# Moving convolutions, weights' products and a PSUM bank in the written order of a hybrid SSD/MLP mixer

## The chip, the core and the metric

The kernel runs on one core of a Trainium2 chip. The metric is the device time of one execution in microseconds (us). Three runs of the kernel before gave 1004.19, 1005.57 and 1009.1 us; their median, 1005.57 us, is the time before. The profile is of one further execution, which took 1003.8 us and whose recorded span is 1002.1 us, at a mean granted TensorE clock of 0.997.

Names of engines in the profile: PE is TensorE's matrix products, PEld its loading of weights, DVE is VectorE, ACT is ScalarE, POOL is GpSimd, SP is SyncE, which issues most DMAs.

## What is computed

One layer of a flow-matching backbone with 256 context tokens and 256 latent tokens, 2048 channels wide. One input projection feeds two groups of heads: a bidirectional Mamba-2 scan (SSD) and a chunked spatial-gating MLP. The part that matters here is the convolved half of the projection and the scan behind it (8 groups of 4 heads, chunks of 128 tokens):

```python
def _dwconv_rows(x, w, b, n_rows, row_len):          # 5 taps
    for k in range(CONV_W):
        y = y + xp[:, :, k:k + row_len] * w[k]
...
    xbc = jax.nn.silu(_dwconv_rows(z[..., :XBC_W], conv_w, conv_b, n_rows, row_len))
...
    states = jnp.einsum('bckgn,bckgr,bckgrp->bcgrpn', Bc, decay_to_end, xdt)
    CB = jnp.einsum('bcqgn,bckgn->bcgqk', Cc, Bc)
    Lmat = jnp.exp(jnp.where(mask, diff, -jnp.inf))
    y_diag = jnp.einsum('bcgqk,bcgrqk,bckgrp->bcqgrp', CB, Lmat, xdt)
    y_off = jnp.einsum('bcqgn,bcgrpn,bcqgr->bcqgrp', Cc, h_starts, jnp.exp(acs))
```

All of it is float32. The context's scans run once to give the start states of the latents' scans, and only latent tokens are put out.

## The kernel before

**Stages.** A prologue (adaLN vectors, RMSNorm, the projection of the time steps and the first seven column tiles) takes about 133 us. Then a loop over `REST` computes the other 25 column tiles of x, B and C, 128 channels each. A tile is numbered by its group and kind: tile 4g and 4g+1 are the two halves of the x channels of group g, 4g+2 is B, 4g+3 is C (C is needed for the latents alone and is 256 columns wide, the others 512). After it comes the "lat" stage, 16 blocks of 512 columns for z, u, v and z of the MLP, and then the output projection.

**Products.** Each float32 product is made of three products of split values (high by high, high by low, low by high). A weight half of 128x1024 arrives by DMA, ACT casts its high part (L414, `hi_w`) and DVE subtracts it to get the low part (L420, `lo_w`), three halves ahead of PE. A column tile takes 48 products (L138 to L140) into one PSUM bank `psx`. These banks come from a pool `acp` of two, in turn: tile n+2 of the loop writes the bank of tile n, once the convolution has read it. All other PSUM tiles come from a pool `sps` of six banks, which gives the bank that has been free longest.

**Convolution.** `conv_tile` makes the first tap on ACT (L479), the others on DVE (L495, eight instructions for a 512-wide tile and four for C), and silu on ACT (L498). Tiles 12, 13 and 15 were projected in the prologue, and wait in SBUF, in segments `zq` of the big buffer `y`; their taps read SBUF (`xbc<-y,...`), where the others read PSUM (`xbc<-psx,...`).

**Scan.** For x halves: `ptx` transposes (L614, PE) and the copy `xk` (L618, ACT); after the second half of a group come the weighted products `xw` (L626, POOL, four) and `xl` (L629, POOL, two), and the skip term (L742, POOL, `y<-xk,dsk`). For B: transposes `ptb` (L637, PE), copy `bk` (L642, ACT). For C: "states" on PE (`pcb` L680, `psc` L697, `psl` L700); `cbb` and `cbf` (L688, L689, DVE); `M` (L725 POOL, then L733 four times on DVE), `E` (L735, DVE), the carried state `hs` (copy L707 on ACT, L713 twice on POOL, `hl` L719 twice on DVE), and then `pso` (L750, PE), which reads `hs`; later `yo` (L756, DVE), `psy` (L776, PE), `pty` (L790, PE). The decays of the next group (L649 `R`, L662 `E` on ACT, with table loads) are queued in the same places. Letter and group are written together below: pso0 is the `pso` of group 0.

**What sets the order.** Every engine's queue stands in written order. Between products, `pump(dt)` advances a virtual clock (1.3 for six wide products, 0.65 for six 256-wide ones), and pieces that `later(dt, fn)` has queued are written when due. `plan_tile(i, src, d0, ds, tx, tw, late)` queues a tile's pieces: convolution at `d0`, silu at `d0 + ds`, transposes at `d0 + tx`; for the second x half `xw` and `xl` at `d0 + tx + tw` and the skip term 3 later; for C the whole list from states on, at `d0 + late` plus fixed offsets:

```python
        if r == 3:
            d0 += late
            for t, fn in [(6, ssd_cb), (6, ssd_states), (6.9, ssd_cbm), (7.6, lambda g: ssd_mb(g, 0)), (8, ssd_hc),
                          (8.7, ssd_hd), (9.4, lambda g: ssd_m(g, 0)), (10.2, ssd_hl), (11.2, lambda g: ssd_mb(g, 1)),
                          (12, ssd_o), (12.2, lambda g: ssd_m(g, 1)), (13.9, lambda g: ssd_yo(g, 0)),
```

The written order ends with block 0 of the lat stage, in which the last group's pieces stand. A block there takes two PSUM banks `pa`, of `acp` in even blocks and of `sps` in odd ones.

Of the kernel before, what the change touches and what calls it, by code (L numbers as in the profile page):

```python
# [8 lines left out]
F32 = mybir.dt.float32  # L9
# [6 lines left out]
P = 128  # L16
# [25 lines left out]
def tile_hybrid_ssd_mlp(  # L42
# [22 lines left out]
    def mkpool(**kw):  # L65
        return tc.tile_pool(reuse_waits="tile", **kw)
# [84 lines left out]
    def yseg(j):  # L151
        return y[:, j // 4, (j % 4) * 512 : (j % 4 + 1) * 512]


    zq = (yseg(2), yseg(3), yseg(7)[:, 0:256])
# [10 lines left out]
    acp = ctx.enter_context(mkpool(name="acp", bufs=2, space=PSUM))  # L166
    sps = ctx.enter_context(mkpool(name="sps", bufs=6, space=PSUM))

    def spt(shape, name):
        return sps.tile(shape, F32, tag="s", name=name)  # L170
# [116 lines left out]
    psx = []  # L287
# [161 lines left out]
    def later(dt, fn):  # L449
        queue.append((now[0] + dt, seq[0], fn))  # L450
        seq[0] += 1
# [14 lines left out]
    def conv_tile(i, src, d0, ds):  # L466
        ch = ORDER[i]
        lat = ch >= 24
        n = 256 if lat else 512
        cw = pc[:, C_CW + 5 * i : C_CW + 5 * i + 5]  # L470
        l0 = 0 if lat else 256
        T = {}

        def tap0():
            if ch < 16:
                o = cv3.tile([P, n], F32, tag="xs", name=f"xbc{i}")
            else:
                o = cv2.tile([P, n], F32, tag="cs" if lat else "bs", name=f"xbc{i}")
            nc.scalar.activation(o, src, AF.Identity, bias=pc[:, C_CB + i : C_CB + i + 1], scale=cw[:, 2:3])  # L479
            T["o"] = o  # L480

        def taps():
            o = T["o"]
            o4 = o[:, l0 : l0 + 256].rearrange("p (r t) -> p r t", r=4)
            src4 = src[:, l0 : l0 + 256].rearrange("p (r t) -> p r t", r=4)
            for k in (0, 1, 3, 4):
                s = k - 2
                parts = [(o4, src4, 64)]
                if not lat:
                    parts.append((o[:, 0:256], src[:, 0:256], 256))  # L490
                for (a, z, w) in parts:
                    o0, o1 = max(0, -s), w - max(0, s)
                    ao = a[..., o0:o1]
                    zi = z[..., o0 + s : o1 + s]
                    nc.vector.scalar_tensor_tensor(ao, zi, cw[:, k : k + 1], ao, op0=ALU.mult, op1=ALU.add)  # L495

        def silu():
            nc.scalar.activation(T["o"], T["o"], AF.Silu)  # L498
            done[i] = T["o"]

        later(d0, tap0)
        later(d0 + 0.9, taps)
        later(d0 + ds, silu)
# [102 lines left out]
    def ssd_x(g, xi):  # L606
        S = gs_.setdefault(g, {})
        if xi == 0:
            S["xk"] = cv2.tile([P, 4, 256], F32, tag="xk", name=f"xk{g}")
        xk = S["xk"]  # L610
        xt = done.pop(4 * g + xi)
        p = spt([P, 4, P], f"ptx{g}{xi}")
        for t in range(4):
            nc.tensor.transpose(p[:, t, :], xt[:, t * P : (t + 1) * P], ident)  # L614
        S["ptx", xi] = p

    def ssd_xc(g, xi):
        nc.scalar.copy(gs_[g]["xk"][:, :, xi * P : (xi + 1) * P], gs_[g]["ptx", xi])  # L618

    def ssd_w(g):  # L620
        S = gs_[g]
        xk, h4 = S["xk"], slice(4 * g, 4 * g + 4)
        xw = cv1.tile([P, 2, 2, 256], F32, tag="xw", name=f"xw{g}")
        for t in range(2):
            for d in range(2):
                nc.gpsimd.tensor_tensor(hp(xw[:, t, d, :]), hp(xk[:, t, :]), bc(wctx(t, d)[:, h4], 2, 64), op=ALU.mult)  # L626
        xl = cv1.tile([P, 2, 256], F32, tag="xl", name=f"xl{g}")
        for d in range(2):
            nc.gpsimd.tensor_tensor(hp(xl[:, d, :]), hp(xk[:, 2 + d, :]), bc(wlt(d)[:, h4], 2, 64), op=ALU.mult)  # L629
        S["xw"], S["xl"] = xw, xl  # L630
# [10 lines left out]
    def ssd_bc(g):  # L641
        nc.scalar.copy(gs_[g]["bk"], gs_[g]["ptb"])  # L642
# [153 lines left out]
    def plan_tile(i, src, d0=0.0, ds=5.2, tx=7.0, tw=1.5, late=0.0):  # L796

        g, r = divmod(i, 4)
        conv_tile(i, src, d0, ds)
        if r < 2:  # L800
            later(d0 + tx, lambda: ssd_x(g, r))
            later(d0 + tx + 0.7, lambda: ssd_xc(g, r))
        if r == 1:
            later(d0 + tx + tw, lambda: ssd_w(g))
            later(d0 + tx + tw + 3, lambda: ssd_sk(g))
        if r == 2:
            later(d0 + tx, lambda: ssd_b(g))
            later(d0 + tx + 0.7, lambda: ssd_bc(g))
# [5 lines that stand above are left out]
                          (14.5, lambda g: ssd_yo(g, 1)), (14.7, lambda g: ssd_ya(g, 0)), (15.3, lambda g: ssd_ya(g, 1)),  # L814
                          (16, ssd_yd), (16.9, ssd_yc), (18.6, ssd_yt), (19.3, ssd_yf)]:
                later(d0 + t, lambda fn=fn: fn(g))
            plan_d(d0 + 11, g + 1, 1.5)
            plan_e(d0 + 17, g + 1)
# [8 lines left out]
    later(2.5, lambda: nc.scalar.copy(zq[2], psx[6]))  # L827
    plan_tile(0, psx[0], 5, ds=7.5, tx=9.5)
    plan_tile(1, psx[1], 12.5, ds=8.5, tx=10)
    plan_tile(2, psx[2], 23.5, ds=7.5, tx=9.5)  # L830
    plan_tile(3, psx[3], 29, ds=5, late=1)
    plan_d(22, 0, 1.5)
    plan_e(27, 0)
    plan_tile(12, zq[0], 76, ds=7, tx=9)
    plan_tile(13, zq[1], 86, ds=7, tx=9)
    for n, i in enumerate(REST):
        lat = ORDER[i] >= 24
        ps = acp.tile([P, 256 if lat else 512], F32, tag="acc", name=f"psx{i}")
        for hf in range(2):
            whi, wlo = half(2 * n + hf)  # L840
            for kk in range(8):
                k = 8 * hf + kk
                w = slice(kk * P, (kk + 1) * P)
                mm3(ps, whi[:, w], wlo[:, w], k, k == 0, k == KT - 1, lat)
                if kk % 2:
                    pump(0.65 if lat else 1.3)
        if i < 8:
            plan_tile(i, ps, ds=7, tx=9, late=10)
        else:
            plan_tile(i, ps)  # L850
        if i == 14:
            plan_tile(15, zq[2], 6, late=10)

# [150 lines left out]
    base = 2 * len(REST)  # L1006
    for blk in range(16):
        kind, j4 = divmod(blk, 4)
        if blk % 2 == 0:
            pa = [acp.tile([P, 512], F32, tag="acc", name=f"pa{blk}{tk}") for tk in range(2)]  # L1010
        else:
            pa = [spt([P, 512], f"pa{blk}{tk}") for tk in range(2)]
        if kind == 1:
            later(3 if j4 == 0 else 0, lambda j4=j4: lat_vn(j4))
            later(10, lambda j4=j4: lat_sg(j4))
        for u in range(8):
            whi, wlo = half(base + blk * 8 + u)
            for kk in range(2):
                k = 2 * u + kk
                w = slice(kk * 512, (kk + 1) * 512)  # L1020
                for tk in range(2):
                    t = slice(256 + tk * P, 256 + (tk + 1) * P)
                    nc.tensor.matmul(pa[tk], lhsT=hhi[k][:, t], rhs=whi[:, w], start=k == 0, stop=False)  # L1023
                    nc.tensor.matmul(pa[tk], lhsT=hhi[k][:, t], rhs=wlo[:, w], start=False, stop=False)  # L1024
                    nc.tensor.matmul(pa[tk], lhsT=hlo[k][:, t], rhs=whi[:, w], start=False, stop=k == KT - 1)  # L1025
                pump(1.3)
            if blk == 0 and u == 7:
                pump(flush=True)
                man.close()
                pos[1] = max(halves) + 1  # L1030
                open_lat()
            if 1 <= blk < 9 and u % 4 == 1:
                gate_tile((blk - 1) * 2 + u // 4)
        if kind == 0:
            later(0, lambda j4=j4, pa=pa: lat_v(j4, pa))
        elif kind == 1:
            later(0, lambda j4=j4, pa=pa: lat_u(j4, pa))
        else:
            later(0, lambda kind=kind, j4=j4, pa=pa: lat_z(kind, j4, pa))
            for pair in range(2):  # L1040
                later(5 + 2 * pair, lambda kind=kind, j4=j4, pair=pair: lat_t(kind, j4, pair))
        if blk == 9:
            later(3, gate_bcast)
# [174 lines left out]
```

## Time and profile before

| what | number |
|---|---|
| median of three runs (lowest, highest) | 1005.57 us (1004.19, 1009.1) |
| profiled execution: time, span | 1003.8 us, 1002.1 us |
| weights' low parts in the loop, L420, DVE | 61 times, 1313 ns each |
| weights' high parts in the loop, L414, ACT | 61 times, 1043 ns each |
| taps from PSUM, L495, DVE | 204, 83.6 us in all |

How to read it: an engine's busy share says how much of the span it worked. A row of the timeline gives start and duration in us, engine, line, operation and tiles, the number of instructions in the row, and in brackets the engine's idle time ahead of it with what ended it. A PE row that begins with idle time in the loop or the lat stage is time in which no product ran.

### The profile page before, as it was taken

How to read it: one execution, taken by the hardware profiler on the slowest of the kernel's cores; microseconds unless marked ns; L12 is line 12 of the kernel's file. 1: busy time of each engine (PE TensorE's matmuls, PEld its weight loads, DVE VectorE, ACT ScalarE, POOL GpSimd, SP SyncE). 2: the span in 40 equal slices, each digit the busy share in tenths (PEclk: the TensorE clock that was granted, in tenths of full speed). 3: DMA queues.
4: the chain of work that ended last, by engine and by line, in shares of the span. 5: the costliest groups of instructions: out<-in, count | busy, mean ns of one | idle time of the engine just before them, and what ended most of it. 6: DMA issues, size and time to landing. Idle time of an engine off the chain costs nothing.

```text
span 1002.1 us, 14182 instructions
## 1 busy us (share of the span) xinstructions
PE 977.1 (98%) x5636; PEld 791.2 (79%) x5636; DVE 624.3 (62%) x944; ACT 492.9 (49%) x759; POOL 111.7 (11%) x162
## 2 busy tenths in 40 slices
PE   8999999999999999999999999999999999999996
PEld 3788887778687878777888888877888888888885
DVE  4344477777877665656667757666555564445546
ACT  4233347555656545544545334454565563446522
POOL 0000003423352222214000000000000000000000
PEclk9999999999999999999999999999999999999998
DMA  9999744233224323134878778674554545556722
GB/s 382 419 412 419 304 159 160 93 127 127 87 82 168 111 100 140 71 126 169 318 279 295 274 260 299 262 280 173 182 191 173 204 168 199 182 208 222 274 92 84
DMA packets 31554, 207.28 MB, mean 207 GB/s; under 512 B 4080, under 2 KB 4208, under 8 KB 7808
## 3 DMA queue, kind: packets, MB, share of 16 engines
q1 hardware_dynamic: 28656, 192.52, 51.1%
q0 software_dynamic: 2112, 12.65, 3.6%
q10 hardware_dynamic: 720, 1.20, 0.3%
q8 instruction: 44, 0.72, 0.3%
q14 instruction: 22, 0.18, 0.1%
HBM read 204.20 MB, written 2.16 MB: 206 GB/s over the span
## 4 chain that ended last, share of the span: by engine, by line
PE 71%; issue 10%; DMA 9%; DVE 7%; ACT 1%; POOL 1%; SPq 0%; DVEq 0%; POOLq 0%; ACTq 0%
PE psx L138 9%; PE psx L140 9%; PE psx L139 9%; PE pa L1023 5%; PE pa L1025 5%; PE pa L1024 5%; DMA gate<-in_wada_dram 5%; PE pm L1072 3%; PE pm L1071 3%; PE pm L1070 3%; PE psada L215 3%; DVE lo_w L82 2%; PE pq L1071 2%; PE pq L1072 2%; PE pq L1070 2%
## 5 line engine op out<-in xcount | busy, mean ns | idle before, releaser
L82 DVE TENSOR_TENSOR lo_w<-w,hi_w 128x1024 fp32r<-128x1024 f32 x173 | 210.1, 1223 | 136.5 <-ACT hi_w L81 136.4
L81 ACT CAST hi_w<-w 128x1024 fp32r<-128x1024 f32 x173 | 182.0, 1052 | 200.7 <-PE pa L1025 130.2
L1023 PE MATMUL pa<-hi_w,hhi 128*128 128x512 f32 x512 | 202.5, 396 | 2.1 <-DVE xbc L495 2.1
L1024 PE MATMUL pa<-lo_w,hhi 128*128 128x512 f32 x512 | 199.4, 390 | 0.1
L1025 PE MATMUL pa<-hi_w,hlo 128*128 128x512 f32 x512 | 199.5, 390 | 0.0
L138 PE MATMUL psx<-hhi,hi_w 128*128 128x512 f32 (+1 forms) x400 | 153.2, 383 | 0.0
L140 PE MATMUL psx<-hhi,lo_w 128*128 128x512 f32 (+1 forms) x400 | 146.0, 365 | 0.0
L139 PE MATMUL psx<-hlo,hi_w 128*128 128x512 f32 (+1 forms) x400 | 145.7, 364 | 0.0
L1023 PEld LDWEIGHTS pa<-hi_w,hhi 128*128 128x128 f32 x512 | 96.1, 188 | 23.1 <-issue 4.1
L1025 PEld LDWEIGHTS pa<-hi_w,hlo 128*128 128x128 f32 x512 | 96.1, 188 | 20.3
L495 DVE SCALAR_TENSOR_TENSOR xbc<-psx,pc,xbc 128x248 f32<-128x248 f32 (+1 forms) x204 | 83.6, 472 | 45.7 <-ACT xbc L479 44.7
L1024 PEld LDWEIGHTS pa<-lo_w,hhi 128*128 128x128 f32 x512 | 96.2, 188 | 19.9 <-DVE lo_w L82 0.5
L420 DVE TENSOR_TENSOR lo_w<-w,hi_w 128x1024 fp32r<-128x1024 f32 x61 | 79.6, 1313 | 21.6 <-ACT hi_w L414 21.6
L138 PEld LDWEIGHTS psx<-hhi,hi_w 128*128 128x128 f32 x400 | 75.5, 189 | 13.3 <-issue 2.8
L140 PEld LDWEIGHTS psx<-hhi,lo_w 128*128 128x128 f32 x400 | 75.4, 189 | 12.6
L139 PEld LDWEIGHTS psx<-hlo,hi_w 128*128 128x128 f32 x400 | 75.6, 189 | 12.0 <-issue 1.4
L414 ACT CAST hi_w<-w 128x1024 fp32r<-128x1024 f32 x61 | 63.5, 1043 | 29.3 <-PE psx L139 15.8
L884 DVE SCALAR_TENSOR_TENSOR junk<-gate,cb 128x2048 bf16<-128x2048 f32 x16 | 36.6, 2290 | 31.2 <-DMA gate<-in_wada_dram 31.1
L1070 PE MATMUL pm<-hi_w,hhi 128*128 128x512 f32 x128 | 49.9, 390 | 0.0
L1071 PE MATMUL pm<-lo_w,hhi 128*128 128x512 f32 x128 | 49.9, 390 | 0.0
L1072 PE MATMUL pm<-hi_w,hlo 128*128 128x512 f32 x128 | 49.7, 389 | 0.0
L138 PE MATMUL psx<-hhi,hi_st 128*128 128x512 f32 (+1 forms) x112 | 41.3, 368 | 0.0
(219 smaller groups left out, 1324.7 us busy)
## 6 DMA issues: line engine op xcount, KB each, us to landing
w<-in_wlat_dram SPq DMA_DIRECT2D x64, 1024.0 KB, 4.8
ada<-in_wada_dram SPq DMA_DIRECT2D x32, 1024.0 KB, 15.2
w<-in_wout_dram SPq DMA_DIRECT2D x32, 1024.0 KB, 4.8
w<-in_wxbc_dram SPq DMA_DIRECT2D x25, 1024.0 KB, 4.8
gate<-in_wada_dram SPq DMA_DIRECT2D x16, 1024.0 KB, 5.7
R<-acs POOLq DMA_DIRECT2D x8, 1024.0 KB, 5.2
wst<-in_wst_dram SPq DMA_DIRECT2D x16, 480.0 KB, 15.5
xT<-in_xch_dram SPq DMA_DIRECT2D x4, 1024.0 KB, 7.8
```

What stands on the lines that cost most here:

```text
L81: nc.scalar.copy(hi, raw)
L82: nc.vector.tensor_tensor(lo, raw, hi.bitcast(F32), op=ALU.subtract)
L138: nc.tensor.matmul(ps, lhsT=whi, rhs=hhi[k][:, s], start=start, stop=False)
L139: nc.tensor.matmul(ps, lhsT=whi, rhs=hlo[k][:, s], start=False, stop=False)
L140: nc.tensor.matmul(ps, lhsT=wlo, rhs=hhi[k][:, s], start=False, stop=stop)
L495: nc.vector.scalar_tensor_tensor(ao, zi, cw[:, k : k + 1], ao, op0=ALU.mult, op1=ALU.add)
L1023: nc.tensor.matmul(pa[tk], lhsT=hhi[k][:, t], rhs=whi[:, w], start=k == 0, stop=False)
L1024: nc.tensor.matmul(pa[tk], lhsT=hhi[k][:, t], rhs=wlo[:, w], start=False, stop=False)
L1025: nc.tensor.matmul(pa[tk], lhsT=hlo[k][:, t], rhs=whi[:, w], start=False, stop=k == KT - 1)
L1070: nc.tensor.matmul(p, lhsT=yh[:, t], rhs=whi[:, w], start=j == 0, stop=False)
L1071: nc.tensor.matmul(p, lhsT=yh[:, t], rhs=wlo[:, w], start=False, stop=False)
L1072: nc.tensor.matmul(p, lhsT=yl[:, t], rhs=whi[:, w], start=False, stop=hf == 0 and j == 15)
```

## The change

Six calls of `plan_tile` get other numbers, and the first two banks of the lat stage come from both pools. Tile 2's transposes are due 2 later; tile 3's list 1 later; tiles 12 and 13 are due 6 earlier and tile 13's transposes 1.5 later after its convolution; the second x half among tiles below 8 that the loop plans, which is tile 5 alone, has its weighted products and skip term 8.2 later; tile 15 is due 2 later. No instruction is added or taken away.

```diff
-    plan_tile(2, psx[2], 23.5, ds=7.5, tx=9.5)
-    plan_tile(3, psx[3], 29, ds=5, late=1)
+    plan_tile(2, psx[2], 23.5, ds=7.5, tx=11.5)
+    plan_tile(3, psx[3], 29, ds=5, late=2)
...
-    plan_tile(12, zq[0], 76, ds=7, tx=9)
-    plan_tile(13, zq[1], 86, ds=7, tx=9)
+    plan_tile(12, zq[0], 70, ds=7, tx=9)
+    plan_tile(13, zq[1], 80, ds=7, tx=10.5)
...
         if i < 8:
-            plan_tile(i, ps, ds=7, tx=9, late=10)
+            plan_tile(i, ps, ds=7, tx=9, tw=9.7, late=10)
...
         if i == 14:
-            plan_tile(15, zq[2], 6, late=10)
+            plan_tile(15, zq[2], 8, late=10)
...
-        if blk % 2 == 0:
+        if blk == 0:
+            pa = [acp.tile([P, 512], F32, tag="acc", name="pa00"), spt([P, 512], "pa01")]
+        elif blk % 2 == 0:
             pa = [acp.tile([P, 512], F32, tag="acc", name=f"pa{blk}{tk}") for tk in range(2)]
```

**POOL at group 0's states.** The rows from group 1's weighted products (`xw`, `xl` and the skip term `y`, all of `xk_1758`) to the second `M` of group 0. Before:

```order
L626 TENSOR_TENSOR xw_1912<-xk_1758,ed 128x256 x4
L629 TENSOR_TENSOR xl_1917<-xk_1758,ed 128x256 x2
L742 TENSOR_TENSOR y<-xk_1758,dsk 128x256 x2
L725 TENSOR_TENSOR M_2018<-cbb_2011,dtt 128x512
L713 TENSOR_TENSOR hs_2028<-hs_2028,ed 128x256 x2
L725 TENSOR_TENSOR M_2063<-cbb_2011,dtt 128x512
```

The same rows of the kernel after:

```order
L725 TENSOR_TENSOR M_2017<-cbb_2013,dtt 128x512
L626 TENSOR_TENSOR xw_2027<-xk_1758,ed 128x256 x4
L629 TENSOR_TENSOR xl_2032<-xk_1758,ed 128x256 x2
L713 TENSOR_TENSOR hs_2025<-hs_2025,ed 128x256 x2
L725 TENSOR_TENSOR M_2071<-cbb_2013,dtt 128x512
L742 TENSOR_TENSOR y<-xk_1758,dsk 128x256 x2
```

Group 0's first `M` passed all of group 1's products, and the skip term went behind group 0's pieces; `hs` still stands behind `xw` and `xl`.

**PE at the same place.** The end of tile 7 (`psx_1903`, 256 wide), group 0's states, and the first products of the next tile, tile 8, which is `psx_1999` before and `psx_1980` after. Before:

```order
L140 MATMUL psx_1903<-hhi_132,lo_w_1801 128x256
L680 MATMUL pcb_1990<-xbc_1883,xbc_1815 128x128 x2
L697 MATMUL psc_1993<-xw_1821,bk_1944 128x512 x2
L700 MATMUL psl_1996<-xl_1826,bk_1944 128x256 x2
L138 MATMUL psx_1999<-hhi_117,hi_w_1855 128x512
```

After:

```order
L140 MATMUL psx_1903<-hhi_132,lo_w_1801 128x256
L138 MATMUL psx_1980<-hhi_117,hi_w_1855 128x512
L139 MATMUL psx_1980<-hlo_133,hi_w_1855 128x512
L140 MATMUL psx_1980<-hhi_117,lo_w_1871 128x512
L138 MATMUL psx_1980<-hhi_118,hi_w_1855 128x512
L139 MATMUL psx_1980<-hlo_134,hi_w_1855 128x512
L140 MATMUL psx_1980<-hhi_118,lo_w_1871 128x512
L680 MATMUL pcb_1991<-xbc_1883,xbc_1815 128x128 x2
```

Six products of tile 8 now stand ahead of the states, which stood directly behind tile 7; the transposes `ptb` of group 0, some way above, moved 18 products down within tile 7.

**DVE at group 2's states.** The rows behind `cbb` and `cbf` of group 2. Before:

```order
L689 TENSOR_TENSOR cbf_2545<-pcb_2528,tri_le 128x256
L733 SCALAR_TENSOR_TENSOR M_2549<-cbf_2545,dtt,M_2549 128x128 x4
L735 TENSOR_TENSOR E_2347<-M_2549,E_2347 128x512
L719 TENSOR_TENSOR hs_2557<-psl_2534,hs_2557 128x256 x2
L495 SCALAR_TENSOR_TENSOR xbc_2582<-psx_2465,pc,xbc_2582 128x4x62
```

After, from the last two of the eight taps of tile 13 on (`xbc_2557`, read from `y`); the eight begin directly behind `cbf`:

```order
L495 SCALAR_TENSOR_TENSOR xbc_2557<-y,pc,xbc_2557 128x4x62
L495 SCALAR_TENSOR_TENSOR xbc_2557<-y,pc,xbc_2557 128x254
L733 SCALAR_TENSOR_TENSOR M_2559<-cbf_2552,dtt,M_2559 128x128 x4
L735 TENSOR_TENSOR E_2347<-M_2559,E_2347 128x512
L719 TENSOR_TENSOR hs_2567<-psl_2535,hs_2567 128x256 x2
```

Tile 13's taps passed group 2's `M`, `E` and `hs`, behind which they stood before.

**ACT there.** From the cast ahead of the copy `hs` of group 2. Before:

```order
L414 CAST hi_w_2526<-w_2341 128x1024
L707 COPY hs_2557<-psc_2531 128x2x256
L498 ACTIVATE xbc_2501<-xbc_2501 128x512
L479 ACTIVATE xbc_2582<-psx_2465,pc 128x512
L414 CAST hi_w_2584<-w_2341 128x1024
```

After:

```order
L414 CAST hi_w_2527<-w_2341 128x1024
L618 COPY xk_2538<-ptx_2539 128x4x128
L479 ACTIVATE xbc_2557<-y,pc 128x512
L707 COPY hs_2567<-psc_2532 128x2x256
L479 ACTIVATE xbc_2599<-psx_2475,pc 128x512
```

The copy `xk` of tile 12 and the first tap of tile 13 passed the copy `hs`; tile 12's silu (`xbc_2501`, `xbc_2434` after) went further up.

## The prediction

> **What bounds the kernel now.** I read the page first, then PE's waits, then the timeline round each wait.
>
> ```profile
> span 1002.1 us, 14182 instructions
> PE 977.1 (98%) x5636; PEld 791.2 (79%) x5636; DVE 624.3 (62%) x944; ACT 492.9 (49%) x759; POOL 111.7 (11%) x162
> ```
>
> PE works 98% of the span, and the change gives it no instruction more or less. So all that can be gained is PE's waits, and a wait removed early is kept to the end, since the engines behind PE are only 11 to 62% busy. The waits of PE (engine, line, what it waited for: us in total, times, longest):
>
> ```profile
> PE ptx L614 <- ACT xbc L498: 2.5, 1, 2.5
> PE pso L750 <- DVE hs L719: 2.2, 2, 2.0
> PE pa L1023 <- DVE xbc L495: 2.1, 1, 2.1
> ...
> PE ptb L637 <- ACT xbc L498: 1.3, 1, 1.3
> ```
>
> These four lines fit the four places of the change: `ptb` of tile 2, pso0, `ptx` of tile 13, and the second bank of the lat stage, pa01. PE's timeline there:
>
> ```profile
> 174.94 0.66 PE L637 MATMUL ptb<-ident,xbc 128*128 128x128 f32 x4 [1.28 <-ACT xbc L498]
> ...
> 188.94 0.39 PE L139 MATMUL psx<-hlo,hi_w 128*128 128x512 f32 x1
> 189.17 0.39 PE L140 MATMUL psx<-hhi,lo_w 128*128 128x512 f32 x1
> 191.53 1.96 PE L750 MATMUL pso<-hs,xbc 128*128 128x512 f32 x4 [1.97 <-DVE hs L719]
> ...
> 269.15 0.66 PE L614 MATMUL ptx<-ident,xbc 128*128 128x128 f32 x4 [2.47 <-ACT xbc L498]
> ...
> 443.83 0.47 PE L1023 MATMUL pa<-hi_w,hhi 128*128 128x512 f32 x1 [2.11 <-DVE xbc L495]
> ```
>
> Idle: 1.28 + 1.97 + 2.47 + 2.11 = 7.83 us. A stop costs a little more than its idle time: products start 0.23 apart (188.94, 189.17), pso0 started 2.36 behind the last, so 2.13 were lost for an idle 1.97, 0.16 more. Four stops lose 7.83 + 4 x 0.16 = 8.5. That is the most that can be gained. The fourth list is whether new waits take their place, so I follow each region through the new order, in the clock of before.
>
> **Region A, 173 to 192 us: ptb0, states, pso0.** `ptb0` stands 18 narrow products later, 18 x 0.12 = 2.1 us, more than its wait: 1.28 + 0.16 go, nothing is late there. But six products of tile 8 now stand ahead of the states, and tile 8's bank is that of tile 6, free when DVE has made tile 6's taps:
>
> ```profile
> 175.59 3.20 DVE L495 SCALAR_TENSOR_TENSOR xbc<-psx,pc,xbc 128x248 f32<-128x248 f32 x8 [2.28 <-ACT xbc L479]
> 178.70 2.35 DVE L420 TENSOR_TENSOR lo_w<-w,hi_w 128x1024 fp32r<-128x1024 f32 x2
> ...
> 181.64 2.01 DVE L495 SCALAR_TENSOR_TENSOR xbc<-psx,pc,xbc 128x248 f32<-128x248 f32 x4
> 183.56 1.37 DVE L420 TENSOR_TENSOR lo_w<-w,hi_w 128x1024 fp32r<-128x1024 f32 x1
> 188.16 1.83 DVE L733 SCALAR_TENSOR_TENSOR M<-cbf,dtt,M 128x128 f32<-128x128 f32 x4 [3.23 <-POOL M L725]
> ```
>
> ```profile
> 179.03 0.61 PE L680 MATMUL pcb<-xbc,xbc 128*128 128x128 f32 x4
> ...
> 181.87 0.58 PE L138 MATMUL psx<-hhi,hi_w 128*128 128x512 f32 x1
> ```
>
> The taps end at 175.59 + 3.20 = 178.79, and nothing in the change moves them, since ACT's first tap stands behind the same work. Before, this was covered: PE took the states at 179.03 and tile 8 at 181.87. After, PE ends tile 7 at 179.03 - 1.44 = 177.6 (its wait at `ptb0` gone) and finds the bank closed until about 178.9: **a new wait of 1.4 (bounds 1.1 to 1.6)**, which gives back what `ptb0` brought. Then six products (1.5), the states (181.87 - 179.03 = 2.84), and 30 products with `ptb1` between (from 181.87 to 189.40 before, 7.5): PE is at pso0 at 190.8.
>
> When is pso0's operand ready? POOL's rows before, then the sum for after:
>
> ```profile
> 181.51 2.33 POOL L626 TENSOR_TENSOR xw<-xk,ed 128x256 f32<-128x256 f32 x4 [9.25 <-PE psc L697]
> 183.81 2.17 POOL L629 TENSOR_TENSOR xl<-xk,ed 128x256 f32<-128x256 f32 x2
> ...
> 188.09 1.23 POOL L713 TENSOR_TENSOR hs<-hs,ed 128x256 f32<-128x256 f32 x2
> ...
> 229.86 1.18 POOL L629 TENSOR_TENSOR xl<-xk,ed 128x256 f32<-128x256 f32 x2
> ```
>
> DVE now takes tile 7's four taps and one low part ahead of `cbb`: 178.79 + 2.3 + 2.0 + 1.3 = 184.4 with `cbb` behind it; `M` on POOL to 185.5; then `xw` 2.33, `xl` and `hs` 1.23. `xl` took 2.17 beside DVE's low part and 1.18 alone, so `hs` ends between 190.25 and 191.25. DVE's last `hl` follows within 0.5 and PE starts 0.1 later: pso0 at 190.9 to 191.85, a wait of 0.1 to 1.05; I take the middle, **0.55**. Region A: 1.44 + 2.13 - 1.4 - 0.55 = 1.8, less 0.2 for two restarts: **1.6 (0.9 to 2.0)**.
>
> [...]
>
> **Region B, 228 to 270 us: tile 12, group 2's states, tile 13.** Tile 12's and tile 13's taps go up DVE's queue. The `ptx` of tile 13 waited for a silu that stood on ACT behind an exponential and a table load (first three rows below); with its taps done by 250 the silu goes ahead of these, some 11 us before PE needs it: 2.47 + 0.16 = 2.63 go. What is late next is pso2, behind ACT's copy `hs` (fourth row):
>
> ```profile
> 266.10 1.06 ACT L662 ACTIVATE E<-E 128x1024 f32<-128x1024 f32 x1 [3.42 <-DVE E L656]
> 267.18 1.28 ACT L498 ACT_TABLE_LOAD   x1
> 268.47 0.63 ACT L498 ACTIVATE xbc<-xbc 128x512 f32<-128x512 f32 x1
> ...
> 243.79 0.59 ACT L707 COPY hs<-psc 128x512 f32<-128x512 f32 x1 [2.69 <-PE psc L697]
> ...
> 253.62 0.59 ACT L618 COPY xk<-ptx 128x512 f32<-128x512 f32 x1 [0.81 <-PE ptx L614]
> 254.10 0.82 ACT L479 ACTIVATE xbc<-y,pc 128x512 f32<-128x512 f32 x1
> ```
>
> ```profile
> 238.85 3.23 DVE L495 SCALAR_TENSOR_TENSOR xbc<-y,pc,xbc 128x248 f32<-128x248 f32 x8 [0.62 <-ACT xbc L479]
> ...
> 246.56 0.69 DVE L735 TENSOR_TENSOR E<-M,E 128x512 f32<-128x512 f32 x1
> 247.18 0.74 DVE L719 TENSOR_TENSOR hs<-psl,hs 128x256 f32<-128x256 f32 x2
> ...
> 253.81 1.13 DVE L733 SCALAR_TENSOR_TENSOR M<-cbf,dtt,M 128x128 f32<-128x128 f32 x4
> ...
> 256.18 4.18 DVE L495 SCALAR_TENSOR_TENSOR xbc<-y,pc,xbc 128x248 f32<-128x248 f32 x8
> ```
>
> ```profile
> 251.27 1.88 PE L750 MATMUL pso<-hs,xbc 128*128 128x512 f32 x4
> ```
>
> `ptx` of tile 12 now stands behind the states and ends at 244.85. ACT copies `xk` to 245.5, makes tile 13's first tap to 246.25 and copies `hs` to 246.7 (before: 244.4). POOL's `hs` follows to 248. DVE's eight taps of tile 13 run from 246.25: 3.23 alone, up to 4.18 beside POOL, so to 249.45 to 250.1 (only two POOL pieces are beside them); then `M` 1.13, `E` 0.69, `hl` 0.74 end at 252.0 to 252.7. PE reaches pso2 at 251.27 + 0.38 for the transposes, 251.65, so **a new wait of 0.4 to 1.1, I take 0.65**, with a restart of 0.1. Before, it had none: pso2 started 0.23 behind the product ahead of it. Behind it stand `psy2` and pso3, with under 1 us of room each: at most 0.3 more, taken at nothing, since they are put off with pso2. Region B: 2.63 - 0.75 = **1.9 (1.5 to 2.2)**.
>
> **Region C, 441 us.** pa00 takes the bank of tile 30, pa01 that of tile 31 so far, and waited for its taps:
>
> ```profile
> 436.13 3.19 DVE L495 SCALAR_TENSOR_TENSOR xbc<-psx,pc,xbc 128x248 f32<-128x248 f32 x8 [3.95 <-ACT xbc L479]
> ```
>
> Tile 30's taps end at 439.3, before PE needs pa00 at 440.87. With pa01 from the other pool (its bank was read by group 6's `yo` long ago) 2.11 + 0.16 = **2.27** go. Five banks are left to group 7's scan: its pieces come one after the other, each wait on a bank would need a tile held over five allocations, and I find none in the new order. Cost nothing; bounds 2.0 to 2.3. Tile 15's shift changes no PE wait that the trace shows: nothing, bounds -0.2 to +0.3.
>
> **Sum.** 1.6 + 1.9 + 2.27 = 5.8 (4.4 to 6.6). Against the profiled execution, 1003.8 - 5.8 = 998.0. The three runs shown are 0.4 to 5.3 above it, their median 1.8; I add 1.0, between the lowest and the median, because one profiled run and the lowest run stand close together: **999.0 us**.
>
> **The rivals.**
>
> - *All waits go and none comes.* For it: PE's order ahead of each wait is looser. Against it: tile 6's taps end at 178.79 whatever comes, and PE will be there at 177.6. It gives 8.5, so 995.3 + 1.0 = 996.3. Chance 0.08.
> - *The new waits are larger.* pso0 and pso2 both take their upper bounds, and one of `psy2` or pso3, whose room is under 1 us, waits as well (0.5 to 1). For it: `M` at 1.83 and the taps at 4.18 beside POOL. It gives 5.8 less 0.5, 0.5 and 0.5 to 1.5: 3.3 to 4.3, so 1000.5 to 1001.5. Chance 0.27.
> - *The change does not do what it says*: each wait comes back in full a few pieces on, since DVE's and ACT's work ahead is the same. Against it: region C's bank is free without any work. With C alone left, 1003.8 - 2.3 + 1.0 = 1002.5. Chance 0.08.
> - *Slower: pso2's chain doubles and the clock drops.* Three serial pieces, ACT's `hs` behind two rows, POOL's `hs` and DVE's `M` behind eight taps, are all slowed by each other. The windows of the end of the span (start to end, length, PE, PEld, DVE, ACT, POOL busy, granted clock, DMA) show the clock falling once PE stops:
>
> ```profile
> 990.00:996.00 6.00, 3.03 (x25) 2.82 (x23) 3.73 (x9) 2.04 (x7) 0.00 (x0) 0.94 0.02 8
> 996.00:1002.00 6.00, 0.00 (x0) 0.00 (x0) 2.50 (x4) 0.00 (x0) 0.00 (x0) 0.50 0.47 175
> ```
>
>   It decides once PE idles longer than 2.47, the longest wait in the loop: a wait of 4 at pso2 in place of 0.65 loses 3.3, and at half the clock 6 us of products take 12. Together 9.3 against the 5.8: 3.5 slower, 1008. Against it: the taps would have to take 6.5 us, and 4.18 is the longest seen. Chance 0.05. [...]
>
> **How the numbers follow.** The forecast has 0.52 (998.2 to 1000.4). About 0.5% (5 us) is what a measurement of this kernel can tell from no change; against 1005.57 that is 1000.5. The forecast and the first rival lie below it but for some 0.05: faster 0.55. The larger waits and the third rival lie within: same 0.41. Slower 0.04. The range runs from 995.8 (all waits gone, with the basis a little lower) to 1003.0 (C alone): it leaves out the slower case and the tails.
>
> **What would show it.** Right: no idle time at `ptb` near 175 or at `ptx` of tile 13; at pa01 none; a wait of some 1.4 at the first product of tile 8, released by DVE's taps; 0.1 to 1 at pso0 and pso2, each by DVE's `hs`. Wrong: no wait at tile 8 (then tile 6's taps came earlier than I think), a wait over 1.5 at pso0 or pso2, or any new one over 0.5 at `pcb`, `psy` or `ptx` between 240 and 300, or in the lat stage where five banks have to do.

## The result, and the profile after

Seven runs of the changed kernel took 998.99 to 1000.08 us, median 999.8; seven of the kernel before 1004.14 to 1009.1, median 1005.95. The ratio is 0.9944, 95% interval 0.9926 to 0.9962. The forecast was 999.0 in a range of 995.8 to 1003.0. The profiled execution took 999.99 us (before: 1003.8), so the two traces account for 3.8 us, and the medians differ by 6.15: where the other 2.3 come from is a question of its own, below.

The page of the kernel after, span and busy time:

```profile
span 998.3 us, 14183 instructions
PE 977.1 (98%) x5636; PEld 791.3 (79%) x5636; DVE 629.9 (63%) x944; ACT 493.0 (49%) x759; POOL 113.7 (11%) x162
```

PE's work is the same to a tenth; DVE's rose by 5.6 us with the same 944 instructions, which the prediction had no term for; 4.3 of it are the four taps of tile 15, shown below. PE's waits after:

```profile
PE pso L750 <- DVE hs L719: 1.8, 3, 1.1
...
PE psx L138 <- DVE xbc L495: 1.3, 1, 1.3
PE ptx L614 <- ACT xbc L498: 1.2, 1, 1.2
...
PE ptm L933 <- DVE vt L993: 0.7, 1, 0.7
```

The line of `pa` and that of `ptb` are gone; `psx` is the new wait of tile 8; `pso` has three waits where it had two; and `ptx` is still there, at half its length. Where they stand, in PE's timeline after (the views end within `pso`, so the second and third row count three and two of its four products):

```profile
179.31 0.47 PE L138 MATMUL psx<-hhi,hi_w 128*128 128x512 f32 x1 [1.26 <-DVE xbc L495]
...
191.78 1.52 PE L750 MATMUL pso<-hs,xbc 128*128 128x512 f32 x3 [0.54 <-DVE hs L719]
...
251.84 1.10 PE L750 MATMUL pso<-hs,xbc 128*128 128x512 f32 x2 [1.07 <-DVE hs L719]
...
274.04 0.66 PE L614 MATMUL ptx<-ident,xbc 128*128 128x128 f32 x4 [1.24 <-ACT xbc L498]
```

The first three are the forecast waits (1.4, 0.55, 0.65). At pso0, DVE's `hl` had itself waited for POOL's `hs`, as forecast:

```profile
190.64 0.99 DVE L719 TENSOR_TENSOR hs<-psl,hs 128x256 f32<-128x256 f32 x2 [1.08 <-POOL hs L713]
```

The fourth wait is not in the forecast: these are the transposes of tile 16, not of tile 13, whose wait is gone. The prediction named a new wait over 0.5 at `ptx` between 240 and 300 as a sign that it is wrong, and this is one. DVE shows what tile 16 waited for, since its taps stand behind those of tile 15:

```profile
260.12 2.36 DVE L656 TENSOR_TENSOR E<-R 128x512 f32<-128x512 f32 x2
262.41 7.15 DVE L495 SCALAR_TENSOR_TENSOR xbc<-y,pc,xbc 128x248 f32<-128x248 f32 x4
269.47 0.68 DVE L794 TENSOR_TENSOR y<-y,pty 128x512 f32<-128x512 f32 x1
270.07 3.19 DVE L495 SCALAR_TENSOR_TENSOR xbc<-psx,pc,xbc 128x248 f32<-128x248 f32 x8
```

Tile 15's four taps took 7.15 us; before they took 2.85:

```profile
262.62 2.85 DVE L495 SCALAR_TENSOR_TENSOR xbc<-y,pc,xbc 128x248 f32<-128x248 f32 x4
```

POOL after, in the stretch of the 7.15 us:

```profile
263.63 2.33 POOL L626 TENSOR_TENSOR xw<-xk,ed 128x256 f32<-128x256 f32 x4
265.93 1.17 POOL L629 TENSOR_TENSOR xl<-xk,ed 128x256 f32<-128x256 f32 x2
267.07 1.18 POOL L742 TENSOR_TENSOR y<-xk,dsk 128x256 f32<-128x256 f32 x2
```

and the view of that one line of the kernel (durations of the four taps in ns, smallest, median, largest):

```profile
L495 DVE SCALAR_TENSOR_TENSOR xbc<-y,pc,xbc x4: 477/714/5140, 262.4 to 269.1; 128x248 f32<-128x248 f32 x2, 128x252 f32<-128x252 f32 x2
```

One tap of the four took 5.14 us, where the shortest took 0.48. It ran from 263.39 to 268.53, so it ended 0.28 us behind the last of POOL's eight instructions, which follow each other without a gap to 268.25. POOL lost nothing: its four `xw` took 2.33, as in five of the eight groups of the kernel before (at 340.54, for one). Three of the kernels below keep this order (both banks from `acp`, tiles 2 and 3 back, tile 5's products behind `hs`), and in each PE waits at a `ptx` as here, 1.2, 1.2 and 1.3 us.

### The profile page after: what moved, and what is told of

It is laid out like the page before. It is cut to its first block, busy times and chain, and to the rows that moved or that the text cites. A ratio compares the mean times of both kernels' runs of the same rounds, so it can differ in the third digit from the quotient of the medians.

```text
span 998.3 us, 14183 instructions
## 1 busy us (share of the span) xinstructions
PE 977.1 (98%) x5636; PEld 791.3 (79%) x5636; DVE 629.9 (63%) x944; ACT 493.0 (49%) x759; POOL 113.7 (11%) x162
## 4 chain that ended last, share of the span: by engine, by line
PE 69%; issue 11%; DMA 9%; DVE 8%; POOL 1%; ACT 1%; SPq 0%; DVEq 0%; POOLq 0%; ACTq 0%
PE psx L138 9%; PE psx L140 9%; PE psx L139 9%; PE pa L1026 5%; PE pa L1028 5%; PE pa L1027 5%; DMA gate<-in_wada_dram 5%; PE pm L1073 3%; PE pm L1075 3%; PE pm L1074 3%; PE psada L215 3%; DVE xbc L495 2%; PE pq L1075 2%; PE pq L1073 2%; PE pq L1074 2%
```

## Experiments

Each kernel is the kernel after with the edit shown, unless said otherwise. Times are medians of 5 to 12 runs, each ratio is against the kernel before on the same chip (it does not go by the medians, so the two can differ a little).

**Tile 15 back.**

```diff
-            plan_tile(15, zq[2], 8, late=10)
+            plan_tile(15, zq[2], 6, late=10)
```

> The kernel after with tile 15's call back at 6 in place of 8; all else as after. What is asked is the wait of 1.24 us at the transposes of tile 16 (near 274 us), which the prediction did not have. Theory (contention): tile 15's four taps, which read SBUF, took 7.15 us because they fell beside the weighted products and the skip term of group 3 on POOL; two places earlier they are done before POOL starts: about 2.0 to 3 us, the wait gone, 1.4 us faster than after (999.8 to 998.4). Rival (chain): tile 16's first tap and its silu are late on ACT whatever tile 15 does: taps shorter, wait still over 0.8, time within 0.5 of after.

Measured: 997.57 us (997.10 to 998.22), ratio 0.9922 (0.9902 to 0.9941). Of the 2.2 us gained, 1.4 are the wait at tile 16, which is gone; the transposes `ptm` of the lat stage, which waited 0.7 in after, do not wait here either, and the other profiles show waits of 0.3 to 0.9 there that come and go. Tiles 12 and 13 keep their new places here, and tile 13's transposes start at 260.58 without a wait, as the prediction told of these places, though tile 15 is back. Tile 15's taps, in DVE's timeline of this kernel:

```profile
261.04 2.86 DVE L495 SCALAR_TENSOR_TENSOR xbc<-y,pc,xbc 128x248 f32<-128x248 f32 x4
```

**POOL's products of group 3 later.**

```diff
-    plan_tile(13, zq[1], 80, ds=7, tx=10.5)
+    plan_tile(13, zq[1], 80, ds=7, tx=15.0)
```

> The kernel after with the transposes of tile 13 later (15.0 in place of 10.5 behind its convolution), so that the copy xk stands behind a further weights' cast on ACT and POOL's weighted products of group 3 start some 4 us later; tile 15's taps stay at their new place. Theory (contention): the taps start near 262.4 as in after and take 2.0 to 3 us in place of 7.15, and the wait of 1.24 at the transposes of tile 16 goes: about 998.4. Rival (the later place alone): taps still late, wait over 0.8 stays, 999.8. A second rival: group 3's states then wait for POOL's products, and give the gain back (wait at psc or psl over 1).

Measured: 997.52 us (997.23 to 999.97), ratio 0.9925 (0.9906 to 0.9943). DVE and POOL:

```profile
262.50 2.49 DVE L495 SCALAR_TENSOR_TENSOR xbc<-y,pc,xbc 128x248 f32<-128x248 f32 x4
```

```profile
268.13 3.31 POOL L626 TENSOR_TENSOR xw<-xk,ed 128x256 f32<-128x256 f32 x4 [4.42 <-ACT xk L618]
```

The taps start where they did (262.5) and take 2.49 once `xw` is not beside them (POOL's earlier `y<-y,yo` runs on to 263.17, beside the first tap, as in after). POOL's DMA issue (L596) stands at 263.12 here and at 263.02 in after, so it is not what made the tap long. The wait at tile 16 is gone and no other came. So it is the neighbour on POOL, not the later place: the rivals fall.

**Both banks from acp again.** The three lines of block 0 taken back.

```diff
-        if blk == 0:
-
-            pa = [acp.tile([P, 512], F32, tag="acc", name="pa00"), spt([P, 512], "pa01")]
-        elif blk % 2 == 0:
+        if blk % 2 == 0:
```

> The kernel after with both banks of the lat stage's first block from the pool acp again. Theory: the wait for tile 31's taps at the second bank comes back, 2.1 idle and 0.16 for the restart: 2.3 slower than after, 1002.1, and nothing else in the trace changes. Rival: five banks in sps cost something in after (a wait that is not seen as one), then under 1.5 slower. Also asked: seven runs of before lie between 1004.1 and 1009.1, seven of after between 999.0 and 1000.1. If that spread comes with the wait of 2.1 us here, the runs of this kernel spread over 3 us or more; if not, about 1.

Measured: median 1001.61 of 12 runs, 1.8 above the kernel after where 2.3 was expected, ratio 0.9968 (0.9955 to 0.9980). The runs lie in two groups with nothing between them: seven from 1001.03 to 1001.69, five from 1003.03 to 1003.51. The profiled execution is one of the upper group (1003.51). The wait is 2.11 again. Windows around it (start to end, length; PE, PEld, DVE, ACT, POOL busy; granted clock; DMA) of this kernel:

```profile
436.00:440.00 4.00, 4.00 (x36) 4.00 (x35) 4.00 (x10) 2.17 (x3) 1.30 (x3) 1.00 0.01 4
440.00:443.50 3.50, 1.39 (x9) 0.95 (x8) 3.31 (x6) 1.50 (x2) 0.00 (x0) 0.98 0.65 236
443.50:447.00 3.50, 3.50 (x9) 2.67 (x10) 0.77 (x1) 0.00 (x0) 0.00 (x0) 0.54 0.59 204
447.00:450.00 3.00, 3.00 (x17) 2.52 (x16) 0.78 (x1) 1.85 (x3) 0.00 (x0) 1.00 0.44 186
```

and of the kernel before, with the same wait:

```profile
443.50:447.00 3.50, 3.17 (x16) 2.69 (x17) 1.32 (x2) 0.40 (x1) 0.00 (x0) 1.00 0.63 215
```

Behind the wait the granted clock is 0.54 for some 3.5 us, and nine products pass where sixteen did: about seven products of 0.23, 1.6 us, against a distance of 2 between the groups. The lower group lies 1.6 above the median of the kernel after and the upper one 3.5: the wait costs somewhat less than its idle time in seven executions and about two more in the other five. That the clock made the two in all five is argued from the one that was profiled.

**Tiles 2 and 3 back.**

```diff
-    plan_tile(2, psx[2], 23.5, ds=7.5, tx=11.5)
-    plan_tile(3, psx[3], 29, ds=5, late=2)
+    plan_tile(2, psx[2], 23.5, ds=7.5, tx=9.5)
+    plan_tile(3, psx[3], 29, ds=5, late=1)
```

> The kernel after with tile 2's transposes back at 9.5 and tile 3's list back at 1; tile 5's weighted products stay late. Theory (the two moves pay for themselves only in part): the wait at ptb of tile 2 comes back (1.28), the wait at tile 8's first product (1.26) goes since the states cover it again, and the wait at pso0 (0.54) goes too, because POOL's hs now stands ahead of xw: 0.5 to 0.8 faster than after, 999.2. Rival (each move is needed): pso0 waits again by over 1 us, as the states' chain is bound by DVE: 1 to 2 slower than after.

Measured: 998.85 us (998.26 to 999.50), ratio 0.9935 (0.9917 to 0.9952), 0.95 faster than after, with the waits as expected (`ptb` 1.29; none at tile 8, none at pso0). With tile 5's products late, the two moves together cost more than they bring: waits of 1.26 and 0.54 in place of one of 1.29.

**Tile 5's products behind hs.**

```diff
-            plan_tile(i, ps, ds=7, tx=9, tw=9.7, late=10)
+            plan_tile(i, ps, ds=7, tx=9, tw=11.0, late=10)
```

> The kernel after with tile 5's weighted products due 1.3 later still (11.0), which on POOL puts the two hs of group 0 ahead of xw and xl; nothing else moves but these. Theory (pso0's wait of 0.54 is POOL's queue: hs ends 191.2 behind xw and xl): the wait goes, 0.7 faster than after, 999.1. Rival (it is DVE: M took 2.56 and E 0.99 beside POOL's xw): M and E are as slow, hl follows them at once near 189.6 and there is still no wait; or, if DVE is slowed further by xl, a wait over 0.3 remains.

Measured: 999.11 us, but over 997.99 to 1000.63, ratio 0.9942 (0.9924 to 0.9959). In the trace the wait at pso0 is gone, though `M` took 2.56 and `E` 0.98 as in after, so POOL's queue was what pso0 waited for. The time does not show it apart from after: three runs lie near 998.1, three near 1000, at the same granted clock (0.996 to 0.998). The profiled execution is of the upper three (999.97). Its granted clock reads 1.00 in every window of the loop and the lat stage (50 to 100 us each). PE waits 0.73 in the lat stage (at 584.81) for a weight's low part, which stands on DVE behind 6.00 us of waiting for the DMA of `gate`; with 0.28 at `ptm` that is about half of the 2 us. No execution of the lower three was profiled, so the rest is open.

**Tiles 12 and 13 back.**

```diff
-    plan_tile(12, zq[0], 70, ds=7, tx=9)
-    plan_tile(13, zq[1], 80, ds=7, tx=10.5)
+    plan_tile(12, zq[0], 76, ds=7, tx=9)
+    plan_tile(13, zq[1], 86, ds=7, tx=9)
```

> The kernel after with tiles 12 and 13 back at 76 and 86 and tile 13's transposes at 9; tile 15 stays at 8. Theory: the wait at tile 13's transposes comes back (about 2.5), the waits at pso2 (1.07) and at tile 16's transposes (1.24, because POOL's products of group 3 are late again) go: by idle time 0.1 to 0.4 faster or slower than after. But the clock: in the run with the old bank the profile shows the granted clock at 0.54 for 3.5 us behind the wait of 2.11, and its times lie in two groups, 1001.0 to 1001.7 and 1003.0 to 1003.5. If a wait of over 2 us lowers the clock in some executions, this kernel's times lie in two groups about 2 us apart as well, its median between 999.5 and 1001.5; if that drop belonged to the lat stage alone, they lie within 1.2 us like those of after.

Measured: 996.37 us (996.24 to 996.54), ratio 0.9914 (0.9897 to 0.9931): 3.4 faster than after. The expectation was wrong in its main point: the wait at tile 13's transposes does not come back. ACT shows why:

```profile
260.51 1.28 ACT L662 ACT_TABLE_LOAD   x1
261.96 1.06 ACT L662 ACTIVATE E<-E 128x1024 f32<-128x1024 f32 x1 [0.17 <-DVE E L656]
263.04 1.28 ACT L498 ACT_TABLE_LOAD   x1
264.34 0.63 ACT L498 ACTIVATE xbc<-xbc 128x512 f32<-128x512 f32 x1
```

Before, the exponential stood at 266.10, after 3.42 us of waiting for DVE's second `E`, which stood behind tile 15's taps. With tile 15 at 8 both `E` are ahead of these taps, and tile 13's silu runs at 264.34 in place of 268.47, in time for PE. So the number of tile 15 is enough to take that wait away, without the new places of tiles 12 and 13. They are enough without it as well: the run with tile 15 back has no such wait either. Both together take it away only once. As no long wait came back, the run says nothing of the clock.

**Tile 13's first tap ahead of the copy xk.**

```diff
-    plan_tile(13, zq[1], 80, ds=7, tx=10.5)
+    plan_tile(13, zq[1], 79.5, ds=7, tx=11.0)
```

> The kernel after with tile 13 due 0.5 earlier (79.5) and its transposes where they were: on ACT its first tap now stands ahead of the copy xk of tile 12, which waits 3.7 us for PE; DVE's order keeps the eight taps ahead of M, E and hl. Theory (pso2's wait of 1.07 comes from the taps starting late behind xk, at 245.3, and not from their number): they start near 242.2, M and hl end by 249.5, the wait at pso2 goes, 1.2 faster than after, 998.6. Rival (the taps ahead of M are too much work wherever they start, POOL slowing them to 4 us): a wait over 0.5 at pso2 remains. In both the wait at tile 16's transposes stays.

Measured: 996.74 us (995.98 to 998.09), ratio 0.9920 (0.9904 to 0.9937). DVE:

```profile
241.93 4.25 DVE L495 SCALAR_TENSOR_TENSOR xbc<-y,pc,xbc 128x248 f32<-128x248 f32 x8
246.10 1.49 DVE L733 SCALAR_TENSOR_TENSOR M<-cbf,dtt,M 128x128 f32<-128x128 f32 x4
...
260.63 2.91 DVE L495 SCALAR_TENSOR_TENSOR xbc<-y,pc,xbc 128x248 f32<-128x248 f32 x4 [0.79 <-ACT xbc L479]
```

The taps are slow as in after (4.25 beside POOL), but start 3.4 us sooner, and the wait at pso2 is gone: it came from their start, behind `xk`. Against the expectation, the wait at tile 16 went too. Tile 15's taps began 1.8 us sooner here, with `xw` starting at 261.16 beside them; this time the four taps took 2.91 together, about the 2.85 of before, and the four `xw` 2.86.

**The new banks alone,** in the kernel before.

> The kernel before with the new banks of block 0 alone (pa01 from sps). Theory: the wait of 2.11 goes and nothing else changes: 2.3 less by the trace's idle time. With the clock drop behind long waits, the waits of 1.97 at pso0 and 2.47 at tile 13's transposes still lower the clock in some executions: times in two or three groups 2 us apart, from 1001 to 1006, median 1002.5 to 1003.5 against 1005.7 of before. Rival (the spread of before has another cause, such as DMA): the spread is that of before, 6 us, or it is gone.

Measured: median 1003.18 of 12 runs, 1.7 below that of the kernel before on this chip, ratio 0.9970 (0.9954 to 0.9985); four runs from 1000.09 to 1000.83 and eight from 1002.82 to 1003.92. The four have a mean granted clock of 0.997, five of the eight one of 0.993 to 0.995, but three of the eight have 0.996 or 0.997, so the clock does not account for the whole upper group. The profiled execution is of the upper group, and shows two stretches at half the clock, behind the waits of 1.96 at pso0 and 2.46 at tile 13's transposes:

```profile
189.00:192.00 3.00, 1.04 (x5) 0.60 (x4) 2.62 (x7) 3.00 (x9) 1.46 (x2) 1.00 0.15 63
192.00:196.00 4.00, 4.00 (x8) 1.91 (x8) 3.75 (x8) 1.69 (x6) 0.28 (x2) 0.57 0.01 4
...
268.00:271.00 3.00, 0.63 (x3) 0.19 (x1) 0.61 (x2) 2.93 (x4) 0.59 (x1) 0.95 0.35 112
271.00:274.00 3.00, 2.90 (x9) 2.52 (x10) 2.26 (x6) 2.44 (x5) 0.48 (x1) 0.50 0.60 243
```

**Four edits of the change, put to use.** The kernel before with tile 2's transposes at 11.5, tile 5's products late, tile 15 at 8 and the new banks; tile 3's list and tiles 12 and 13 as before.

```diff
-    plan_tile(2, psx[2], 23.5, ds=7.5, tx=9.5)
+    plan_tile(2, psx[2], 23.5, ds=7.5, tx=11.5)
...
-            plan_tile(i, ps, ds=7, tx=9, late=10)
+            plan_tile(i, ps, ds=7, tx=9, tw=9.7, late=10)
...
-            plan_tile(15, zq[2], 6, late=10)
+            plan_tile(15, zq[2], 8, late=10)
```

> The kernel before with four of the edits: tile 2's transposes at 11.5, tile 5's weighted products late, tile 15 at 8, the new banks; tile 3's list stays at 1 and tiles 12 and 13 where they were before. Theory (the parts each do what the last runs show, and add up): no wait at tile 2's ptb; the states directly behind tile 7 wait about 0.5 for the copy bk, but cover tile 8's bank; hs stands ahead of xw on POOL, so none at pso0; none at tile 13's transposes, at tile 16's, nor at pso2. That is e6 (996.4) less 1.4 + 0.7 plus 0.6: 994.9, and one group of times, since no wait is over 1.3. Rival (the states' new place was needed): pso0 or the states wait by over 1, no better than 996.4.

Measured: 996.05 us (995.46 to 996.23), ratio 0.9912 (0.9897 to 0.9927). The states cost even less than expected (0.14 at `pcb`, next to nothing at `psc`), but pso0 still waits 0.59, which was not expected: DVE's `M` took 2.57 and `E` 0.98 beside POOL's `xw`. So the time is 1.15 above the expected 994.9, and no better than can be told from the 996.37 with tiles 12 and 13 back (ratios 0.9912 and 0.9914).

**Tile 15 alone,** in the kernel before.

> The kernel before with tile 15's call at 8 in place of 6, nothing else. Theory (from the run with tiles 12 and 13 put back): this one number takes the wait of 2.47 at tile 13's transposes away, because both of the decays' E now stand ahead of tile 15's taps on DVE, so that the exponential and the table load behind it are off ACT some 3 us sooner; 2.6 less than before by idle time, the waits of 1.97 and 2.11 stay and with them some executions at a lower clock: median 1001.5 to 1003, in groups 2 us apart. Rival (tiles 12 and 13 or the new bank were needed as well): the wait at tile 13's transposes stays over 1.5, median within 1 us of before.

Measured: median 1002.1 of 12 runs (999.79 to 1003.77), ratio 0.9970 (0.9958 to 0.9982). The wait at tile 13's transposes is gone from PE's rows, those of 1.97 and 2.11 stay. The times spread over 4 us, without clear groups.

**POOL's xw and xl behind the second M,** on top of the four edits.

```diff
-            plan_tile(i, ps, ds=7, tx=9, tw=9.7, late=10)
+            plan_tile(i, ps, ds=7, tx=9, tw=13.0, late=10)
```

> The kernel of the last run (996.05) with tile 5's weighted products due 3.3 later still (13.0), so that POOL makes xw and xl behind group 0's second M. What is asked is the wait of 0.59 left at pso0, where DVE's four M took 2.57 and E 0.98 beside POOL's xw. Theory (M and E read two SBUF operands and are held up by POOL's xw): with POOL idle beside them M takes 1.1 to 1.3 and E 0.7, hs is ready near 188.2 and the wait goes: 995.3. Rival (M is late because the third low part stands ahead of it, and is long of itself): M over 2, the wait over 0.4 stays, 996.0. Second rival: group 1's states then wait for xw, over 0.7, and the time is no better.

Measured: 994.79 us (994.41 to 995.27), ratio 0.9893 (0.9875 to 0.9910): the fastest of all, 5.0 below the kernel after, and 1.26 below the kernel with the four edits, more than the 0.75 of the wait and its restart. DVE at group 0's `M`, first and second:

```profile
185.09 1.13 DVE L733 SCALAR_TENSOR_TENSOR M<-cbf,dtt,M 128x128 f32<-128x128 f32 x4
186.26 0.69 DVE L735 TENSOR_TENSOR E<-M,E 128x512 f32<-128x512 f32 x1
...
188.17 2.54 DVE L733 SCALAR_TENSOR_TENSOR M<-cbf,dtt,M 128x128 f32<-128x128 f32 x4 [0.55 <-POOL M L725]
190.74 0.98 DVE L735 TENSOR_TENSOR E<-M,E 128x512 f32<-128x512 f32 x1
```

The first `M`, now alone, takes 1.13, and the second, beside `xw`, 2.54: the same work, with and without the neighbour, in one execution. Nothing near waits for the second. Among PE's waits none of the loop is left over 0.2 us.

## Why the forecast came out as it did

**Region C was right.** 2.11 and the restart were forecast to go with nothing in return; they went, and came back when the bank was taken back. By the medians this is worth 1.7 to 1.8, where 2.27 was forecast.

**Region A was right in its steps, with a slip in its sum.** Forecast: the wait at tile 8 of 1.4 and at pso0 of 0.55. Measured: 1.26 and 0.54. The sum 1.44 + 2.13 - 1.4 - 0.55 is 1.62 and not 1.8, so that the region comes to 1.4, the whole forecast to 5.6 and the time to 999.2. What the region brought can be read from rows that stand at the same place in both orders: tile 6's taps start at 175.59 before and at 175.97 after, group 2's `ptb` at 236.88 and at 235.77. That is 0.38 + 1.11, or 1.5. The mechanism of pso0 was also as told (POOL's queue), shown by the run that put `hs` ahead of `xw`. What the prediction did not ask is whether the moves of tiles 2 and 3 were worth making together: with both taken back, the kernel is 0.95 faster.

**Region B brought nothing, -0.1 in place of 1.9.** In the kernel after, group 2's `ptb` starts 1.11 sooner than before, but group 4's only 0.97 sooner (303.60 and 304.57), so 0.14 was lost between them, tile 15's shift included. The wait of tile 13's transposes went as told (2.47), and pso2 and tile 16 took it back. For pso2 the prediction was right but for the size. The term "a new wait of 0.4 to 1.1, I take 0.65" was mis-sized: it measured 1.07. The taps took 3.94 in place of the 3.23 to 4.18 that I gave half of, so the bound from the taps beside POOL was the nearer one. The chain was the forecast one, and the experiment shows which link decides: the taps wait for their first tap behind `xk`, and taps that start 3.4 us earlier let pso2 through though they are no shorter (4.25).

**The step that failed is "Tile 15's shift changes no PE wait that the trace shows: nothing, bounds -0.2 to +0.3".** It cost 1.24 idle and a restart, 1.4. I had followed the place of tile 15's taps on DVE, not what POOL would be doing beside them: the earlier copy `xk` of tile 13 started POOL's eight instructions there, and one tap beside them took 5.14 us. In the other direction I missed a benefit of the same shift: by itself it removes the wait of tile 13's transposes, as the run with that one edit shows. So beside it the earlier places of tiles 12 and 13 brought only the waits at pso2 and tile 16.

**The sum, and two errors that met.** From 1003.8 the forecast took 5.8. The trace took 3.8: region A 1.5, region B -0.1, what lies behind it 2.8 (2.27 for region C, the rest small waits of the lat stage, such as `ptm`), less 0.4 that was lost ahead of region A. Then I added 1.0 for the distance of the profiled execution from the median. For the kernel after that distance is -0.2 (999.99 against 999.8). So 2.0 too much was taken away and a basis 1.2 too high was added, and that 999.0 came within 0.8 of 999.8 is partly luck. The distance before belonged to its long waits, as far as the runs tell. Two runs that keep one or two of them show the clock at 0.50 to 0.57 for some 3 to 4 us in their profiled execution, and times about 2 us apart; the profiled execution of before has all three waits and the clock at 1.00 behind each (its windows from 192 to 196, 270 to 274 and 443.5 to 447), so no drop is in it, while before's runs over all these comparisons spread from 1002.74 to 1010.5. Sixty of these runs of before have their mean granted clock noted, and the time goes with it: the eleven at 0.997, like the profiled one, took 1002.74 to 1004.86 (median 1003.26), the eleven at 0.990 or 0.991 took 1007.08 to 1009.1 (median 1007.5). The clock is not the whole of it, since one at 0.998 took 1005.93; and no execution of before with a drop was profiled.

**The rivals.** "The new waits are larger" named pso2's bound rightly, and the further wait came at a place it did not name. The slower rival had the clock fall once PE idles longer than 2.47, a limit that no run shows: behind an idle time of 1.96 the clock read 0.57 in one execution, behind one of 2.47 it read 1.00 in another, and what decides was not shown. By the spread of the runs the lower clock spoke for the change, which cut the longest wait of the loop from 2.5 to 1.3: the seven runs of after lie within 1.1 us, the seven of before within 5.0.

## What to carry to other kernels

Where a piece is moved, ask for each engine what the others will be doing beside it, not only what stands ahead of it: one tap on DVE took 5.14 us here beside eight instructions of GpSimd, where the shortest of the same four took 0.48. Of a change made of several numbers, test each number alone: here one of six was enough for the main benefit of a region, two that brought the same benefit a second time added only waits, and leaving these two out was worth more than half of what the whole change gained. A wait of PE of 2.11 us cost 1.6 us here in seven executions and 3.5 in five, of which the one profiled shows the clock at 0.54 behind the wait; a single profiled execution can miss that.

## What the runs showed of the hardware

**DVE and POOL side by side.** DVE's four `M` took 1.13 with POOL idle and 2.54 to 2.57 beside `xw`. POOL's four `xw` took 2.33 in five of the eight groups of the kernel before, and 3.49 beside a low part and `M` of DVE in the kernel with the four edits. One tap took 5.14 beside eight POOL instructions in a row, though in another run the four taps of the same tile took 2.91 in all with `xw` (2.86) beside them. Why the durations differ so, no run shows. By its recorded start the tap of 5.14 was first (263.39, `xw` 263.63), and it ended behind the last of the eight all the same (268.53, 268.25). That one tap can last as long as a whole run of the other engine's instructions I had not expected, and what decides between that and the 2.91 for four stays open.

**The clock behind short waits.** Idle times of 1.96 and 2.46 us (the new banks alone) and of 2.11 us (both banks from `acp`) were each followed, in the profiled execution, by windows of 3 to 4 us at a granted clock of 0.50 to 0.57, shown with these runs. In the profiled execution of before, idle times of 1.97, 2.47 and 2.11 us at the same places were followed by windows at 1.00. The first two with the windows behind them (columns as above; the third is shown with the banks from `acp`):

```profile
188.00:192.00 4.00, 2.03 (x8) 1.24 (x7) 3.25 (x8) 4.00 (x13) 2.36 (x4) 1.00 0.26 107
192.00:196.00 4.00, 4.00 (x16) 2.77 (x15) 3.97 (x8) 1.41 (x5) 0.38 (x1) 1.00 0.01 4
...
266.00:270.00 4.00, 1.53 (x10) 1.03 (x9) 0.86 (x3) 3.87 (x5) 0.59 (x1) 1.00 0.41 176
270.00:274.00 4.00, 4.00 (x20) 3.26 (x18) 4.00 (x9) 2.13 (x5) 2.42 (x4) 1.00 0.22 90
```

So waits of about the same length were followed by a lower clock in one execution and not in another; what decides was not shown. In the profiled execution of after, whose longest wait in the loop is 1.26, the clock reads 1.00 in every window up to 980 us (50 to 100 us each).

Some kernels whose longest wait in the loop is 1.3 us or less had single runs 1.2 to 2.6 above their group (999.97 against 997.4 with POOL's products later, three of six with tile 5's products at 11.0), at granted clocks no lower than the rest. The one that was profiled shows part of a cause, the late low part behind the DMA of `gate`; the rest stays open.
